# A fused two-group decoder step: the second half of the prompt laid out as the first, and a planner that prices DMA packets and queue slots

## The chip, the cores and the metric

One core of one Trainium2 chip. The time is the device time of one execution in microseconds, the median of the runs shown.

## What is computed

One decoder layer (`DEPTH` is 1) for two groups of requests that share weights: a prompt of 1024 rows and eight single sampled rows with 512 past positions each. Width 1024, feed-forward width 2816, all float32.

```
h = x + 0.5 * rmsnorm(swiglu(rmsnorm(x), gate1, up1, down1))
P = rmsnorm(h) @ w_in                    # 1024 -> 3328 columns
ya = differential attention, 4 heads     # columns 0..1535 of P: q, k, v, rotary on 16 of 64 dims
yb = RWKV-7 time mixing, 8 heads of 64   # columns 1536..3327: token shift, decay, matrix state, group norm
h = h + rmsnorm(concat(ya, yb) @ w_out)
y = h + 0.5 * rmsnorm(swiglu(rmsnorm(h), gate2, up2, down2))
```

The sampled rows attend over a paged cache (`cache_k[page_table]`, `cache_v[page_table]`) and carry their own RWKV state; beside the two `y` the kernel returns the new keys, values, states and last projected rows.

## The kernel before

The prompt is cut into two halves of 512 columns; the eight sampled columns ride along in phase 0 and in phase 3 (520 columns each, the other two phases 512). The feed-forward work is a **trunk** of four phases: phase 0 is FFN 1 of the first half, phase 1 FFN 1 of the second half, phase 2 FFN 2 of the first half, phase 3 FFN 2 of the second half. Between FFN 1 and FFN 2 of a half lies its mixer: the projection `w_in` (stream `proj`, 26 weight tiles), four RWKV jobs (`job`, two at a time), the attention (`prep`, `attn`, `fin`), and `w_out` (`out` for the first half, `outb` for the second). So the mixer of the first half runs beside the trunk of phase 1, and that of the second half beside the trunk of phase 2. The sampled rows have two decoders of their own: `dec` (attention over the cache) and then `decb` (RWKV step).

Every float32 product is three matmuls in fp32r: the weights and the activations are split into a high part and the rest (`split`, `pair`, `mm3`). A weight tile therefore comes in by one 512 KB DMA on SP, is cast by ScalarE, and VectorE or GpSimd subtracts the cast from the original (`wts_w`, `lin_w`). In phases 0 and 3 the trunk has four weight tiles and most gate/up products go by a seven-product scheme on blocks (`sums`, `seven`); in phases 1 and 2 it has two, `w0` and `w1`, and the RWKV jobs use `w2`, `w3`.

The order of the instructions on each engine is made by a **planner** in the program itself. Each stream is a generator (`s_trunk`, `s_weights`, `s_project`, `s_job`, ...) that puts operations into queues; `Kern.put` works out what each depends on, `Kern.price` gives a cost, and `Kern.run` (from L481) picks the next operation: of those ready first, the one with the earliest due time. Due times come from `latest`, which goes backwards over the last plan. `kernel` makes `PASSES` plans in a dry run, takes the one with the shortest planned time, and emits it; the engines then run their instructions in this order. `BIAS = {"trunk2": 300}` sets all due times of the trunk's phase 2 300 us later.

The tiles that the change is about:

- `dreg` (4160 floats a partition): the cache pages and scratch of `dec`, then all scratch of `decb`, later the low halves of the second half's attention operands (`a_buffers`). In phase 1 it also holds the activations of the first `LEAD` = 4 trunk tiles.
- `xl0`, `xl1`: `xl1` is the ring of the trunk's activations, `xl0` the sum of its down products (`self.ytile`).
- `T0`, `T1`: normed input of phases 1 and 3; RWKV job buffers and attention operands of the second half. `X0`, `X1` are the same for the first half.
- `T2`, `T3`: staging tiles (`stage`).

**How the first half is laid out** (s_weights, s_trunk, s_tail, s_project; phase 0 to 1). The residual is read ahead into a free tile (`s_resid`), the normed output goes to `T2`/`T3`, and the operand of the projection to `xl0`/`xl1`. That is possible since phase 1 starts with four gate/up tiles whose activations go to `dreg`; they fill TensorE while the tail is worked out. Then the weight stream stops: the 26 tiles of `w_in` take `w0`, `w1`, and the trunk goes on after them, with a new ring in `xl1`. The job buffers `X0`, `X1` are free at once, so jobs start beside the projection. The first decoder waits for `lead`, the point in phase 1 (group 2, after the down products of group 1) from which `dreg` is free.

**How the second half is laid out.** The residual comes by `hres` DMAs inside the tail (`post`, from L809), the tail works in place in `xl0`, and the operand of the projection goes to `T0`/`T1`. The weights of `w_in` go through `lraw`/`LT` to `w2`, `w3`, beside the trunk of phase 2, which goes on in its ring from its first tile. The job buffers of the second half are the same `T0`, `T1`, so `s_mix` waits for `proj1` (the end of the projection) before it gives them out (L1557). `decb` starts once `dec` is through and has `dreg` from then on. The second half's attention waits for the jobs, the rotary step and `dec_b`, the end of `decb`.

`wide` is true in phases 1 and 2; `cut(t, 4)` makes four places for activations of a tile `t`; `places` names the weight tiles of a linear stream and what frees them.

Of the kernel before, what the change touches and what calls it, by code (L numbers as in the profile page):

```python
# [22 lines left out]
P = 128  # L23
# [72 lines left out]
PASSES = 4  # L96
BIAS = {"trunk2": 300}
# [118 lines left out]
class Kern:  # L216
# [167 lines left out]
    def price(o, op, a, k, out, ins):  # L384
# [5 lines left out]
        if "dma" in op:  # L390
# [9 lines left out]
            o.dma = n * out.shape[0] * 4 / run * max(run * (1 + (run < 512)), 157) / 360e3  # L400
# [80 lines left out]
    def run(self):  # L481
# [4 lines left out]
        rings, tile, size, credit, paced = 0.0, None, None, 0.0, 0.0  # L486
        while self.streams:
# [321 lines left out]
    def post(self, rb, y, gain, o, z=None, rs=None, res=None):  # L809
# [4 lines left out]
        for k in range(KT):  # L814
            if rs is None and k % 2 == 0:
                r = self.residual(n)
                nc.sync.dma_start(r, (self.res if res is None else res)[:, k:k + 2, o:o + n])
# [42 lines left out]
    def s_weights(self):  # L860
# [3 lines left out]
        for ph in range(4):  # L864
# [152 lines left out]
    def s_trunk(self):  # L1017
# [3 lines left out]
        for ph in range(4):  # L1021
# [11 lines left out]
            act = cut(self.T(self.pool, [P, W_DEC], "dreg", FR), 4) if ph == 1 else cut(ring, 4)  # L1033
# [28 lines left out]
            def up(f, c):  # L1062
# [117 lines left out]
            for gi, grp in enumerate(groups):  # L1180
                for q, f in enumerate(grp):
# [11 lines left out]
                    if ph == 1 and f == LEAD:  # L1193
# [49 lines left out]
    def s_tail(self, ph, c, acc, y):  # L1243
# [25 lines left out]
        self.post(norm, y, f"n_ffn{1 + ph // 2}_post", h0 + o, z, rs, self.I["xT"] if ph == 1 else None)  # L1269
        self.signal(("posted" if c else "post", ph))  # L1270
        if ph < 2:
            for t, k in ((self.ytile, 0),) if ph else ((self.zt[0], 0), (self.zt[1], 4)):
                self.keep(ph, c, t, k)
            y = z or y
# [1360 lines left out]
```

## Time and profile before

| | us |
|---|---|
| median of 3 runs | 2288.88 |
| lowest, highest | 2285.25, 2290.93 |
| profiled execution, its own time | 2291.46 |
| span of its profile, first to last instruction | 2289.5 |
| TensorE (PE) busy | 2211.9 (97%) |
| VectorE (DVE) busy | 1539.8 (67%) |
| ScalarE (ACT) busy | 1084.8 (47%) |
| GpSimd (POOL) busy | 977.3 (43%) |
| mean granted TensorE clock | 0.984 |

The first lines of a window table are the stretch in us, its length, and then for each engine the busy time with the number of instructions; then the granted TensorE clock (1 is full speed), the busy share of the 16 DMA engines and what they moved. All operations have the line of one helper (L323), so the tiles' names tell the work: `proj_m<-tail_T,lin_w` is a matmul of the projection into a PSUM bank of the `m` set, with operand `tail_T` and weight `lin_w`. A timeline row has the start, the length, the engine, the operation, and in square brackets how long the engine had been idle and what ended that.

### The profile page before, as it was taken

The numbers are of one execution on the slowest core, as the hardware profiler recorded it, in microseconds if no ns is written. First come the engines' busy times: TensorE is split into PE (matmuls) and PEld (weight loads), VectorE is DVE, ScalarE is ACT, GpSimd is POOL, SyncE is SP. The second block draws the span as 40 slices with busy tenths as digits, with TensorE's granted clock in tenths as the row PEclk, the third lists the DMA queues.
The fourth block names the chain that finished last, engine by engine and source line by source line (L and its number), as shares of the span: only waits on it lengthen the run. The fifth ranks groups of instructions, "written<-read, shape, count | busy, mean of one in ns | idle before, by whom it ended". The sixth has DMA issues, their size and how long they took to land.

```text
span 2289.5 us, 42336 instructions
## 1 busy us (share of the span) xinstructions
PE 2211.9 (97%) x15671; PEld 1970.4 (86%) x15671; DVE 1539.8 (67%) x3573; ACT 1084.8 (47%) x2233; POOL 977.3 (43%) x818
## 2 busy tenths in 40 slices
PE   8999998999999899999899999999999979999998
PEld 8999998898887677988787877777788879999998
DVE  7748887746676587378657566655676356777775
ACT  6524344644553455443552255543576465544444
POOL 4525555533332665464442123333453254444443
PEclk9999999999999999999999999989999989999999
DMA  7322233444343656455568643423644847433433
GB/s 256 109 93 93 84 111 121 135 147 125 110 118 108 177 170 223 138 191 172 162 199 218 184 148 113 111 74 114 196 123 132 278 144 258 152 112 119 148 139 112
DMA packets 241799, 338.75 MB, mean 148 GB/s; under 512 B 78970, under 2 KB 160314, under 8 KB 241594
## 3 DMA queue, kind: packets, MB, share of 16 engines
q1 hardware_dynamic: 241306, 335.53, 46.8%
q8 instruction: 124, 2.03, 0.4%
q14 instruction: 81, 0.66, 0.1%
q10 hardware_dynamic: 288, 0.52, 0.1%
HBM read 281.01 MB, written 54.98 MB: 147 GB/s over the span
## 4 chain that ended last, share of the span: by engine, by line
PE 80%; DVE 7%; DMA 5%; ACT 4%; issue 2%; POOL 1%; SPq 1%; DVEq 0%; ACTq 0%; POOLq 0%
PE trunk_m L323 46%; PE proj_m L323 12%; PE trunk_aux L323 8%; PE job_aux L323 5%; PE out_m L323 2%; PE outb_m L323 2%; PE attn_m L323 2%; DVE mix_T L323 2%; PE attn_aux L323 1%; ACT mix_T L323 1%; SPq L323 1%; PE job_dec L323 1%; DVE trunk_xl L323 1%; PE job_cb L323 1%; DMA mix_T<-out_dram 1%
## 5 line engine op out<-in xcount | busy, mean ns | idle before, releaser
L323 POOL TENSOR_TENSOR wts_w<-wts_raw,wts_w 128x1024 fp32r<-128x1024 f32 (+2 forms) x154 | 293.0, 1909 | 439.0 <-ACT wts_w L323 390.0
L323 PE MATMUL trunk_m<-trunk_xl,wts_w 128*128 128x256 f32 (+2 forms) x2700 | 459.7, 321 | 8.1 <-DVE trunk_xl L323 7.7
L323 PE MATMUL trunk_m<-pre_X,wts_w 128*128 128x512 f32 (+3 forms) x2400 | 441.1, 336 | 12.7 <-ACT wts_w L323 5.5
L323 PEld LDWEIGHTS trunk_m<-trunk_xl,wts_w 128*128 128x128 f32 x2700 | 381.5, 189 | 43.4 <-DVE trunk_xl L323 5.6
L323 PEld LDWEIGHTS trunk_m<-pre_X,wts_w 128*128 128x128 f32 x2400 | 354.1, 191 | 54.7 <-DVE trunk_g L323 6.0
L323 PE MATMUL trunk_m<-pre_T,wts_w 128*128 128x512 f32 (+3 forms) x1848 | 361.8, 349 | 7.7 <-DVE trunk_xl L323 7.7
L323 ACT CAST wts_w<-wts_raw 128x1024 fp32r<-128x1024 f32 (+3 forms) x299 | 244.6, 834 | 217.5 <-PE trunk_m L323 131.7
L323 PEld LDWEIGHTS trunk_m<-pre_T,wts_w 128*128 128x128 f32 x1848 | 291.6, 193 | 46.1 <-issue 9.0
L323 DVE TENSOR_TENSOR trunk_xl<-trunk_xl,trunk_m 128x256 f32<-128x256 f32 (+2 forms) x351 | 165.5, 490 | 60.4 <-PE trunk_m L323 59.1
L323 PE MATMUL proj_m<-tail_xl,lin_w 128*128 128x256 f32 (+1 forms) x1248 | 164.9, 288 | 0.0
L323 PE MATMUL proj_m<-tail_T,lin_w 128*128 128x512 f32 (+1 forms) x672 | 151.7, 384 | 8.9 <-DVE tail_T L323 6.3
L323 PEld LDWEIGHTS proj_m<-tail_xl,lin_w 128*128 128x128 f32 x1248 | 153.5, 188 | 7.7 <-issue 6.4
L323 PEld LDWEIGHTS proj_m<-tail_T,lin_w 128*128 128x128 f32 x672 | 122.3, 193 | 36.4 <-DVE tail_T L323 7.1
L323 POOL TENSOR_TENSOR trunk_xl<-trunk_t,trunk_xl 128x512 fp32r<-128x512 f32 (+3 forms) x85 | 89.0, 1048 | 150.2 <-ACT trunk_xl L323 149.8
L323 DVE TENSOR_TENSOR wts_w<-wts_raw,wts_w 128x1024 fp32r<-128x1024 f32 (+3 forms) x115 | 117.2, 1024 | 26.1 <-ACT wts_w L323 21.6
L323 POOL TENSOR_TENSOR lin_w<-lin_raw,lin_w 128x1024 fp32r<-128x1024 f32 x22 | 53.7, 2442 | 106.5 <-ACT lin_w L323 93.5
L323 ACT CAST wts_w<-wts_lraw 128x512 fp32r<-128x512 f32 x94 | 55.7, 619 | 68.0 <-DMA wts_lraw<-in_ffn_down_dram 34.4
L323 DVE TENSOR_TENSOR trunk_t<-trunk_g,trunk_m 128x512 f32<-128x512 f32 (+2 forms) x75 | 42.1, 562 | 59.1 <-PE trunk_m L323 52.3
L323 POOL TENSOR_TENSOR wts_w<-wts_lraw,wts_w 128x512 fp32r<-128x512 f32 x43 | 59.8, 1392 | 44.8 <-ACT wts_w L323 39.7
L323 DVE SCALAR_TENSOR_TENSOR trunk_g<-trunk_t,trunk_m 128x512 f32<-128x512 f32 (+2 forms) x52 | 32.4, 624 | 61.5 <-ACT trunk_t L323 61.2
L323 PE MATMUL trunk_aux<-trunk_xl,wts_w 128*128 128x256 f32 (+1 forms) x516 | 71.3, 283 | 0.0
L323 PE MATMUL trunk_m<-comb_T,wts_w 128*128 128x260 f32 x540 | 69.7, 283 | 0.0
(619 smaller groups left out, 4196.8 us busy)
## 6 DMA issues: line engine op xcount, KB each, us to landing
wts_raw<-in_ffn_gate_dram SPq DMA_DIRECT2D x87, 512.0 KB
wts_raw<-in_ffn_up_dram SPq DMA_DIRECT2D x58, 512.0 KB
wts_raw<-in_ffn_down_dram SPq DMA_DIRECT2D x56, 384.0 KB
wts_raw<-in_ffn_down_dram SPq DMA_DIRECT2D x29, 512.0 KB
lin_raw<-in_w_in_dram SPq DMA_DIRECT2D x26, 512.0 KB
wts_w<-Ld SPq DMA_DIRECT2D x22, 512.0 KB
mix_T<-out_dram SPq DMA_DIRECT2D x36, 256.0 KB
Ld<-wts_w SPq DMA_DIRECT2D x24, 384.0 KB
```

What stands on the lines that cost most here:

```text
L323: o = Op(eng, lambda: fn(*a, **k), st)
```

## The change

In the second half, what differed from the first is made the same, by turning conditions on phase 0 or 1 into conditions on both halves:

- the residual of phase 1's tail is read ahead by `s_resid`; the tail works into `T2`/`T3` (after phase 2's input is staged) and puts the projection's operand into `xl0`/`xl1`;
- phase 2 starts with four gate/up tiles into `dreg`, after a new wait for `dec_a`, the end of `dec`; the weight stream then waits until the last `w_in` tile is loaded, and the trunk goes on with a new ring in `xl1`; its first down products wait for `proj1`;
- `s_project` of the second half uses `w0`, `w1` and the trunk's two `raw` tiles, after the fourth up tile is loaded; it no longer waits for `outw`;
- `s_mix` gives out the job buffers of the second half without a wait for `proj1`;
- `decb` additionally waits for `lead2`, the point of phase 2 that `lead` (now `lead1`) is in phase 1.

In the planner, a DMA costs `9 + 0.041 * run` nanoseconds for each packet of `run` bytes on one of 16 engines; an operation of SP with a DMA can't start before one of eight places is free, and holds it until 0.1 us after landing; `BIAS` is emptied, and `PASSES` goes from 4 to 8.

```diff
-PASSES = 4
-BIAS = {"trunk2": 300}
+PASSES = 8
+BIAS = {}
...
-            o.dma = n * out.shape[0] * 4 / run * max(run * (1 + (run < 512)), 157) / 360e3
+            o.dma = n * out.shape[0] * 4 / run * (9 + 0.041 * run) / 16e3
...
+        lanes = deque([0.0] * 8)
...
-                        c.append((max(free[e], o.ready + o.load, held[OTHER[e]] if o.port else 0.0), st.prio[e] if o.late is None else o.late, o))
+                        c.append((max(free[e], o.ready + o.load, held[OTHER[e]] if o.port else lanes[0] if o.dma and e != "gpsimd" else 0.0), st.prio[e] if o.late is None else o.late, o))
...
                 o.seen = rings + LAND
+                if o.eng != "gpsimd":
+                    lanes.append(o.seen + 0.1)
+                    lanes.popleft()
...
-                if ph == 1 and n == 2 * LEAD:
-                    yield ("wait", ("loaded", ("in", 0), 25))
-                    last |= {tag: ("used", ("in", 0), 24 + i) for i, tag in enumerate(tags)}
+                if ph in WIDE and n == 2 * LEAD:
+                    yield ("wait", ("loaded", ("in", ph - 1), 25))
+                    last |= {tag: ("used", ("in", ph - 1), 24 + i) for i, tag in enumerate(tags)}
...
-            act = cut(self.T(self.pool, [P, W_DEC], "dreg", FR), 4) if ph == 1 else cut(ring, 4)
+            if ph == 2:
+                yield ("wait", "dec_a")
+            act = cut(self.T(self.pool, [P, W_DEC], "dreg", FR), 4) if wide else cut(ring, 4)
...
-                        if ph == 0:
+                        if ph < 2:
                             self.spawn(self.s_resid(ph), "resid", 0)
...
-                    if ph == 1:
-                        yield ("wait", "proj0")
+                    if wide:
+                        yield ("wait", f"proj{ph - 1}")
...
-                    if ph == 1 and f == LEAD:
+                    if wide and f == LEAD:
                         ring = self.T(self.big, [P, 4160], "xl1", FR)
...
-                        if ph == 1 and gi == 2:
-                            self.signal("lead")
+                        if wide and gi == 2:
+                            self.signal(f"lead{ph}")
...
-        if ph == 0:
+        if ph < 2:
             yield ("wait", ("resid", ph))
             rs = self.rs[c][0]
             if c == 0:
+                if ph:
+                    yield ("wait", ("staged", 2))
                 self.zt = self.stage()
...
-                if ph == 0:
-                    yield ("wait", ("posted", 0))
-                self.px = self.parts(ph, *(self.two(1) if ph else [self.T(self.big, [P, 4160], f"xl{j}", FR) for j in range(2)]))
+                yield ("wait", ("posted", ph))
+                self.px = self.parts(ph, *[self.T(self.big, [P, 4160], f"xl{j}", FR) for j in range(2)])
...
-        if half:
-            yield ("wait", ("outw", 0))
-        else:
-            yield ("wait", ("loaded", 1, "up", LEAD - 1, None))
-            places = ("w0", "w1"), [("used", 1, kind, LEAD - 1, None) for kind in ("gate", "up")]
+        yield ("wait", ("loaded", 1 + half, "up", LEAD - 1, None))
+        places = ("w0", "w1"), [("used", 1 + half, kind, LEAD - 1, None) for kind in ("gate", "up")]
...
-            if half:
-                yield ("wait", "proj1")
             self.job_buffers(half, j)
...
+        self.signal("dec_a")
 
     def s_decode_b(self):
         yield ("wait", "proj0")
+        yield ("wait", "lead2")
```

More of the change, by code (lines that the diff above doesn't have):

```diff
@@ L807, in residual, with post @@
         return r.rearrange("p (j t) -> p j t", j=2)
-    def post(self, rb, y, gain, o, z=None, rs=None, res=None):
+    def post(self, rb, y, gain, o, z=None, rs=None):
         z = z or y
@@ L816, in post @@
                 r = self.residual(n)
-                nc.sync.dma_start(r, (self.res if res is None else res)[:, k:k + 2, o:o + n])
+                nc.sync.dma_start(r, self.res[:, k:k + 2, o:o + n])
             nc.vector.scalar_tensor_tensor(z[k], y[k], self.vec(gain, k), rb, ALU.mult, ALU.mult)
@@ L1256, in s_tail @@
             if c == 0:
+                if ph:
+                    yield ("wait", ("staged", 2))
                 self.zt = self.stage()
             z = [a + b for a, b in self.parts(ph, *self.zt)][c]
-        else:
+        if ph:
             for what in (f"jobs0_{ph - 1}", f"jobs1_{ph - 1}", f"rope{ph - 1}"):
@@ L1268, in s_tail @@
             nc.vector.tensor_tensor(norm, norm, rb, ALU.mult)
-        self.post(norm, y, f"n_ffn{1 + ph // 2}_post", h0 + o, z, rs, self.I["xT"] if ph == 1 else None)
+        self.post(norm, y, f"n_ffn{1 + ph // 2}_post", h0 + o, z, rs)
         self.signal(("posted" if c else "post", ph))
         if ph < 2:
-            for t, k in ((self.ytile, 0),) if ph else ((self.zt[0], 0), (self.zt[1], 4)):
+            for t, k in ((self.zt[0], 0), (self.zt[1], 4)):
                 self.keep(ph, c, t, k)
-            y = z or y
+            y = z
             if c:
@@ L1445, in s_project @@
         nc = self.nc
-        places = None
         for c in range(2):
             yield ("wait", ("prb", half, c))
-        if half:
-            yield ("wait", ("outw", 0))
-        else:
-            yield ("wait", ("loaded", 1, "up", LEAD - 1, None))
-            places = ("w0", "w1"), [("used", 1, kind, LEAD - 1, None) for kind in ("gate", "up")]
+        yield ("wait", ("loaded", 1 + half, "up", LEAD - 1, None))
+        places = ("w0", "w1"), [("used", 1 + half, kind, LEAD - 1, None) for kind in ("gate", "up")]
         job = [16, 12, 20]
@@ L1943, in s_decode_a @@
         yield ("wait", ("done", 0, 3))
-        yield ("wait", "lead")
+        yield ("wait", "lead1")
         if SWAP:
@@ L1951, in s_decode_a @@
             self.spawn(self.s_decode_b(), "decb", 1, "dec", ahead=8)
+        self.signal("dec_a")
     def s_decode_b(self):
         yield ("wait", "proj0")
+        yield ("wait", "lead2")
         if SWAP:
             yield ("wait", "setup")
-            yield ("wait", "lead")
+            yield ("wait", "lead1")
         take = self.arena(self.T(self.pool, [P, W_DEC], "dreg"))
```

## The prediction

> **What bounds the kernel now.** I read the page's busy row and chain first, then a window table cut at the borders of the stages, then the timeline where that table showed idle time.
>
> ```profile
> span 2289.5 us, 42336 instructions
> PE 2211.9 (97%) x15671; PEld 1970.4 (86%) x15671; DVE 1539.8 (67%) x3573; ACT 1084.8 (47%) x2233; POOL 977.3 (43%) x818
> ```
>
> TensorE is the bound on the whole, and the change takes no matmul away. So it can win only what TensorE loses: idle time, and busy time at a lower granted clock. The window table has both (first pair of numbers: length and PE busy; after the POOL column the granted clock, then the DMA share). The first four rows are the first half's layout, the next seven the second half's and what follows it.
>
> ```profile
> 355.00:405.00 50.00, 43.80 (x324) 42.14 (x323) 35.96 (x77) 21.23 (x41) 21.90 (x23) 0.93 0.40 131
> 435.00:655.00 220.00, 218.64 (x2027) 201.40 (x2026) 139.33 (x446) 101.48 (x185) 73.74 (x58) 1.00 0.42 126
> 655.00:745.00 90.00, 88.53 (x712) 68.87 (x710) 54.49 (x168) 41.58 (x96) 27.92 (x23) 1.00 0.40 115
> 745.00:890.00 145.00, 131.77 (x652) 102.78 (x651) 109.00 (x233) 74.70 (x204) 95.34 (x64) 0.96 0.62 188
> 1100.00:1150.00 50.00, 40.30 (x297) 38.16 (x296) 31.36 (x62) 28.12 (x58) 23.47 (x27) 0.90 0.55 175
> 1150.00:1330.00 180.00, 179.14 (x846) 146.69 (x845) 107.18 (x154) 59.70 (x81) 51.49 (x36) 1.00 0.67 189
> 1203.00:1291.00 88.00, 88.00 (x385) 70.38 (x384) 64.34 (x86) 21.89 (x25) 23.68 (x13) 1.00 0.87 223
> 1330.00:1500.00 170.00, 163.56 (x1195) 126.28 (x1194) 117.95 (x391) 93.35 (x185) 62.63 (x40) 1.00 0.44 127
> 1500.00:1615.00 115.00, 112.69 (x785) 88.01 (x784) 60.42 (x181) 46.23 (x102) 35.91 (x25) 0.93 0.32 92
> 1615.00:1866.00 251.00, 248.68 (x1479) 212.73 (x1478) 145.77 (x319) 151.31 (x363) 102.06 (x75) 1.00 0.61 192
> 1866.00:1925.00 59.00, 43.63 (x307) 41.68 (x306) 38.09 (x73) 34.14 (x65) 30.95 (x44) 0.83 0.48 160
> 1925.00:2262.00 337.00, 337.00 (x2806) 336.95 (x2805) 251.09 (x533) 149.91 (x311) 147.26 (x140) 1.00 0.41 145
> ```
>
> I count a row's loss as idle time plus busy time times the missing clock. Second half: border into phase 2 (1100:1150) 9.7 + 0.10 x 40.3 = 13.7; projection and jobs (1150:1330, 1330:1500, 1500:1615) 0.9 + 6.4 + 2.3 + 0.07 x 112.7 = 17.5; attention and `w_out` 2.3; border into phase 3 (1866:1925) 15.4 + 0.17 x 43.6 = 22.8. Together 56.3 us. Phase 3 itself has none. The first half: border 6.2 + 0.07 x 43.8 = 9.3; projection and jobs 1.4 + 1.5 = 2.9.
>
> The timeline shows what the borders wait for.
>
> ```profile
> 1127.97 2.40 PE L323 MATMUL trunk_m<-trunk_xl,wts_w 128*128 128x256 f32 x18 [0.21 <-DVE trunk_xl L323]
> 1132.90 0.38 PE L323 MATMUL proj_m<-tail_T,lin_w 128*128 128x256 f32 x1 [2.53 <-ACT tail_T L323]
> 1139.55 7.75 PE L323 MATMUL proj_m<-tail_T,lin_w 128*128 128x256 f32 x45 [6.27 <-DVE tail_T L323]
> ```
> ```profile
> 1879.01 1.22 PE L323 MATMUL stats_dec<-bset_bv,init_onesD 128*128 128x256 f32 x2 [7.92 <-DVE bset_bv L323]
> 1883.22 8.30 PE L323 MATMUL trunk_m<-pre_X,wts_w 128*128 128x256 f32 x48 [2.99 <-DVE trunk_g L323]
> ```
> ```profile
> 1916.60 8.78 PE L323 MATMUL trunk_m<-pre_T,wts_w 128*128 128x264 f32 x48 [3.23 <-DVE trunk_xl L323]
> ```
>
> At 1130.4 phase 1 is over, and TensorE waits for the tail's operand `tail_T`. At 1871 phase 2 has one tile left and TensorE waits for the statistics of the second half's `w_out` result: the chain jobs, attention, `w_out`, norm ends at the same time as the trunk that should cover it.
>
> **The change part by part.**
>
> *Border into phase 2.* Four gate/up tiles now stand between the last down product and the projection, as in the first half. Its row prices it: 9.3 in place of 13.7, **-4.4**. The residual's 2 MB come ahead of the tail beside the last down weights, by four DMAs on SP in place of these eight; the first half's row holds that too.
>
> ```profile
> tail_hres<-in_xT_dram SPq DMA_DIRECT2D x8, 256.0 KB
> ```
>
> The new wait for `dec_a` I cost at nothing. Queued behind it are the whole of phase 2's trunk and, through the weight stream, the projection; TensorE would have only the tail left.
>
> ```profile
> 1100.81 0.25 DVE L323 SCALAR_TENSOR_TENSOR dec_dreg<-dec_dreg,init_cols 128x32 f32<-128x32 f32 x1
> ```
>
> `dec` is through with `dreg` at 1101, 29 us before phase 2 starts at 1130.4. If that cover goes, every microsecond of it is one of the total.
>
> *Projection and jobs.* The jobs lose the wait for `proj1` and run beside the projection, as in 435:655. Loss 2.9 in place of 17.5, **-14.6**. Against it stands that the first half's projection took longer beside its jobs:
>
> ```profile
> L323 PE MATMUL proj_m<-tail_xl,lin_w 128*128 128x256 f32 (+1 forms) x1248 | 164.9, 288 | 0.0
> ```
> ```profile
> L323 PE MATMUL proj_m<-tail_T,lin_w 128*128 128x512 f32 (+1 forms) x672 | 151.7, 384 | 8.9 <-DVE tail_T L323 6.3
> ```
>
> 13.2 us more, of which 2.4 are its 520 columns against 512. The trunk tiles that the jobs leave may win the other 10.8 back, so the cost is 0 to 10.8; I take the middle, **+5.4**.
>
> *The second decoder* moves from beside the projection to beside phase 2's trunk after `lead2`. No row shows that pairing. Below: 1203:1291, its own core at a DMA share of 0.87, lost nothing. Above: 745:890, `dec` beside trunk and attention, lost 13.2 + 0.04 x 131.8 = 18.5 in 145 us, 17 for 136 us of `decb`. The instructions are those of the first row, so I take **+4**.
>
> *Border into phase 3.* Where the chain comes earlier than the trunk does, the waits of 7.92 and 2.99 and their low clock go; what stays is the last wait, 3.23, and about as much for the clock behind it: 6.6 in place of 22.8, **-16.2** at most.
>
> So TensorE's own limit is -4.4 - 14.6 + 5.4 + 4 - 16.2 = **-26**.
>
> *The chain.* It must come earlier by as much, or TensorE idles at the end instead. This is the step to look at, since the change puts `decb` into it: the attention's operands need `dreg`.
>
> ```profile
> 383.71 3.00 PE L323 MATMUL trunk_m<-pre_T,wts_w 128*128 128x256 f32 x24
> ```
> ```profile
> 434.95 0.40 PE L323 MATMUL proj_m<-tail_xl,lin_w 128*128 128x256 f32 x2
> ```
> ```profile
> L323 PE MATMUL trunk_m<-trunk_dreg,wts_w x96: 387/396/505, 654.7 to 736.5; 128*128 128x512 f32 x96
> ```
> ```profile
> 1233.14 76.45 PE proj_m L323 x330
> ```
>
> In the first half the projection starts 51.2 us after the trunk's phase, so now at 1130.4 + 51.2 = 1181.6. `dreg` was last read 301.6 us after that, which gives 1483. But in the 82 us from 654.7 to 736.5 the trunk needed only 216 matmuls (`plan`: down groups 0 and 1 with 72 and 48, two gate/up pairs with 96) at the projection's 76.45 / 330 = 0.232 us each, 50 us; the other 32 were the jobs', and then nothing waited for `dreg`. Now due times put the trunk first: 1483 - 32 = 1451.
>
> ```profile
> 1102.97 0.37 SPq L323 DMA_DIRECT2D decb_dreg<-out_dram  x1
> ```
> ```profile
> 1133.15 0.22 ACT L323 ACTIVATE decb_dreg<-decb_dreg 128x32 f32<-128x32 f32 x1
> ```
> ```profile
> 1149.40 0.30 PE L323 MATMUL decb_dec<-decb_dreg,init_bones 128*128 128x32 f32 x2
> ```
> ```profile
> 1153.46 0.19 DVE L323 TENSOR_TENSOR decb_dreg<-decb_dreg,init_cols 128x32 f32<-128x32 f32 x1
> ```
> ```profile
> 1200.32 0.30 PE L323 MATMUL decb_dec<-decb_dreg,init_bones 128*128 128x32 f32 x2
> ```
> ```profile
> 1290.82 0.69 DVE L323 TENSOR_REDUCE decb_dreg<-decb_dreg 128x8 f32<-128x512 f32 x1
> ```
> ```profile
> 1326.29 0.30 PE L323 MATMUL decb_dec<-decb_dreg,init_bones 128*128 128x32 f32 x2
> ```
> ```profile
> 1336.25 0.38 SPq L323 DMA_DIRECT2D YM<-decb_dreg  x1
> ```
>
> `decb` took 1103.0 to 1336.6, 234 us. Three times its next matmul, which needed nothing but the row before, came late: 16, 47 and 35 us. Nothing was waiting for it then. Without them it is 136 us.
>
> ```profile
> L323 PE MATMUL job_aux<-bset_sg,bset_g x8: 592/592/675, 1437.2 to 1612.9; 128*128 128x512 f32 x8
> ```
> ```profile
> 1618.39 0.48 PE L323 MATMUL attn_aux<-mix_T 128*128 128x320 f32 x2
> ```
>
> The attention started 5.5 us after the last job. Now: 1451 + 136 + 5.5 = 1592.5, **26 us earlier** than 1618.4. The jobs are no limit: from the end of the projection at 1330 they took 283 us, and as long from 30 us into the projection they end near 1495. Both limits come out at 26. Where they meet, each still delays the other; I give back a good third of the 10.9 us of waits at 1871 to 1883, 4 us: **-22**.
>
> *The plan.* Four more passes and the empty `BIAS` cost no instruction. The new order reaches the whole program, but 1925:2262 has nothing left to win; for the rest I allow 8 us either way, a little over half of the 13.2 idle in 745:890. The packet price can be checked on the stretch of `decb`:
>
> ```profile
> DMA packets 33484, 19.59 MB, mean 223 GB/s; under 512 B 29329, under 2 KB 29361, under 8 KB 33478
> ```
> ```profile
> q1 hardware_dynamic: 33478, 19.51, 86.5%
> ```
>
> Measured: 0.865 x 88 = 76.1 us of each engine. New price: (33478 x 9 + 19.51e6 x 0.041) / 16 = 68.8 us. The plan thus takes this stretch, nearly all packets of 256 bytes, for 7 us shorter than it is. The Trainium skill ("DMA: Bandwidth & Descriptors", Specifications) says that below 512 bytes the engines do a read-modify-write and miss line rate, which is the step that the old price had and the new one drops; by that rule, and this row agrees in sign, the attention starts some 7 us later than planned and the gain would be 15 in place of 22.
>
> **The rivals.**
>
> *No change.* The trunk keeps the first half's pace to `lead2`, and only `decb` hurries: 1483 + 136 + 5.5 = 1624.5, 6 us later than now. What TensorE saves at 1130 and 1500 is then idle time at 1870, and the time is 2289 + 6 = 2295. For it: the pace is a measured one. Against it: then nothing waited for `dreg`.
>
> *Slower: the decoder is last.* `decb` starts at 1451 but keeps two of its late matmuls, since each is one in a queue of trunk matmuls and its result goes through a busy VectorE: 136 + 16 + 35 = 187, attention at 1643.5, 25 us later, and the end with it: 2314. It decides from a `decb` of 169 us on (1618.4 + 7 - 5.5 - 1451). For it: the change ties a step of many small DMAs and short vector work, which had 1618 - 1337 = 281 us to spare, into the only chain that ends at phase 3. Against it: the plan knows that and sets its due times by it.
>
> *The layout does less than it says*: the first half's clean rows came from its plan and not from the layout, and the second half's jobs, in step with each other, lose the clock again as in 1500:1615: 7.9 of the 14.6 stay. The chain still comes 26 earlier: about 2275, inside my range.
>
> **How the numbers follow.** The profiled execution took 2291.5, 2.6 above the median of 2288.9; I apply -22 to the median: **2267**. Chances: the forecast with its variants 0.60, no change 0.17, decoder last 0.23. The likeliest case's own range is 2246 (no cost of `decb`, nothing given back, 8 from the new order: -42) to 2281. The whole range goes on through the no-change case to 2306, short of the slower case's 2314 and what lies above it, some 0.12; below 2246 I leave 0.06. A measurement tells 0.3%, about 7 us, from no change: faster 0.60, same 0.17, slower 0.23.
>
> **What would show it.** Right: no wait for `tail_T` at 1130 to 1150; job matmuls from about 1210 on among the projection's; `trunk_m<-trunk_dreg` a second time, ending near 1451; `decb` right after it, done near 1590; the attention's first matmul near 1593; no wait over 5 us before phase 3. Wrong: `decb` over 169 us, a gap of TensorE before phase 3 longer than now, the first activation of phase 2 waiting for `dec_dreg`, or a clock below 1 between 1181 and 1500.

## The result and the profile after

| | median, us | lowest to highest | runs |
|---|---|---|---|
| before | 2289.9 | 2285.25 to 2294.97 | 4 |
| after | 2262.68 | 2260.26 to 2266.19 | 4 |

The ratio is 0.9882 (95% interval 0.9856 to 0.9907): 27 us less. The first two lines of the page of after, then its window table, cut at its own borders of the stages (length and TensorE busy first; after the POOL column the granted clock):

```profile
span 2261.8 us, 42336 instructions
...
PE 2204.0 (97%) x15671; PEld 1961.9 (87%) x15671; DVE 1561.4 (69%) x3583; ACT 1078.3 (48%) x2222; POOL 983.4 (43%) x817
```
```profile
745.00:890.00 145.00, 138.45 (x703) 109.58 (x702) 111.65 (x244) 77.98 (x210) 99.87 (x64) 1.00 0.67 199
1100.00:1170.00 70.00, 66.96 (x412) 59.16 (x411) 51.48 (x80) 41.57 (x78) 41.37 (x44) 1.00 0.62 212
1170.00:1360.00 190.00, 188.91 (x1247) 146.41 (x1245) 117.93 (x303) 85.43 (x153) 69.28 (x40) 1.00 0.42 130
1360.00:1452.00 92.00, 88.70 (x661) 69.94 (x659) 66.87 (x228) 44.44 (x98) 26.11 (x17) 1.00 0.46 133
1452.00:1582.00 130.00, 129.84 (x685) 101.11 (x684) 82.44 (x169) 44.67 (x78) 41.27 (x24) 1.00 0.67 171
1582.00:1755.00 173.00, 171.29 (x954) 142.02 (x953) 128.27 (x266) 107.40 (x292) 75.24 (x45) 1.00 0.49 148
1755.00:1840.00 85.00, 84.99 (x556) 77.20 (x556) 36.12 (x61) 42.97 (x72) 32.71 (x34) 1.00 0.79 268
1840.00:1896.00 56.00, 42.36 (x309) 39.98 (x308) 37.81 (x74) 34.51 (x66) 28.81 (x42) 0.88 0.46 149
```

TensorE's idle time fell from 77.6 (2289.5 - 2211.9) to 57.8 us (2261.8 - 2204.0), its busy time by 7.9: 19.8 + 7.9 = 27.7, the whole difference of the spans. From 1100 to 1840 only 9.3 us are lost in all; two thirds of what is left of the second half's losses are in the last row, the border into phase 3: 13.6 idle + 0.12 x 42.4 = 18.7 us. And 745:890, in a stage whose layout the change does not touch, loses 6.6 where it lost 18.5.

The timeline at the two borders of after, first into phase 2, then into phase 3:

```profile
1111.73 4.56 PE L323 MATMUL trunk_m<-trunk_xl,wts_w 128*128 128x256 f32 x37
1116.13 0.59 PE L323 MATMUL tail_aux<-trunk_acc,init_onesD 128*128 128x256 f32 x2
1117.37 2.86 PE L323 MATMUL trunk_m<-pre_X,wts_w 128*128 128x256 f32 x22 [0.64 <-ACT wts_w L323]
```
```profile
1872.51 7.48 PE L323 MATMUL trunk_m<-trunk_xl,wts_w 128*128 128x256 f32 x45 [7.14 <-DVE trunk_xl L323]
1880.20 4.53 PE L323 MATMUL trunk_m<-trunk_xl,wts_w 128*128 128x256 f32 x36 [0.21 <-DVE trunk_xl L323]
1884.57 0.59 PE L323 MATMUL last_aux<-trunk_acc,init_onesD 128*128 128x256 f32 x2
1884.81 2.48 PE L323 MATMUL trunk_m<-trunk_xl,wts_w 128*128 128x256 f32 x18
1889.71 7.47 PE L323 MATMUL trunk_m<-pre_T,wts_w 128*128 128x264 f32 x47 [2.42 <-DVE trunk_xl L323]
```

Phase 2 begins 0.6 us after phase 1; no wait for the tail is left. Phase 3 begins at 1889.7 in place of 1916.6, 26.9 earlier, with a wait of 7 us a little ahead of it. The chain that leads there:

```profile
L323 PE MATMUL trunk_m<-trunk_dreg,wts_w x96: 387/393/798, 1376.8 to 1451.5; 128*128 128x512 f32 x96
```
```profile
1451.91 0.38 SPq L323 DMA_DIRECT2D decb_dreg<-out_dram  x1
```
```profile
1581.50 0.43 SPq L323 DMA_DIRECT2D YM<-decb_dreg  x1
```
```profile
1582.82 0.48 PE L323 MATMUL attn_aux<-mix_T 128*128 128x320 f32 x2
```
```profile
L323 PE MATMUL outb_m<-outb_T,lin_w x384: 275/283/475, 1754.7 to 1834.6; 128*128 128x264 f32 x96, 128*128 128x256 f32 x96
```

`dreg` is read for the last time at 1451.5, `decb` starts 0.4 us later and ends at 1582, the attention starts there, and `w_out` at 1754.7. The attention starts 35.6 us earlier than before, but `w_out` only 23.6. The trunk's share of TensorE in the attention's stretch shows where the 12 us between the two went (length, then busy time of the trunk's products alone; before, then after):

```profile
1618.40:1778.30 159.90, 106.74 (x395) 71.14 (x394) 18.40 (x27) 2.96 (x5) 1.00 0.51 154
```
```profile
1582.80:1754.70 171.90, 119.16 (x447) 80.58 (x446) 19.81 (x29) 3.57 (x6) 1.00 0.49 147
```

What is not trunk is the same, 53.2 and 52.7 us: the attention lasted 12 us longer, and TensorE did 12 us more of the trunk in it. TensorE is busy in nearly the whole stretch, so this does not show which caused which. Trunk products may have stood ahead of the attention's, or have filled its waits for another engine (VectorE's busy time in the stretch rose from 110.5 to 127.3 us).

### The profile page after: what moved, and what is told of

Its sections match the earlier page's. It is cut to its first block, busy times and chain, and to the rows that moved or that the text cites. A ratio compares the mean times of both kernels' runs of the same rounds, so it can differ in the third digit from the quotient of the medians.

```text
span 2261.8 us, 42336 instructions
## 1 busy us (share of the span) xinstructions
PE 2204.0 (97%) x15671; PEld 1961.9 (87%) x15671; DVE 1561.4 (69%) x3583; ACT 1078.3 (48%) x2222; POOL 983.4 (43%) x817
## 5 line engine op out<-in xcount | busy, mean ns | idle before, releaser
L323 PE MATMUL trunk_m<-trunk_xl,wts_w 128*128 128x256 f32 (+2 forms) x2604 | 433.7, 318 | 14.5 <-DVE trunk_xl L323 11.9
L323 PE MATMUL trunk_m<-pre_X,wts_w 128*128 128x512 f32 (+3 forms) x2400 | 430.2, 333 | 9.3 <-ACT wts_w L323 6.5
L323 PEld LDWEIGHTS trunk_m<-trunk_xl,wts_w 128*128 128x128 f32 x2604 | 366.2, 190 | 44.4 <-DVE trunk_xl L323 13.5
L323 PEld LDWEIGHTS trunk_m<-pre_X,wts_w 128*128 128x128 f32 x2400 | 353.1, 190 | 49.7 <-ACT wts_w L323 5.9
L323 PE MATMUL proj_m<-tail_xl,lin_w 128*128 128x256 f32 (+2 forms) x1920 | 327.2, 323 | 0.4 <-POOL lin_w L323 0.4
L323 PEld LDWEIGHTS proj_m<-tail_xl,lin_w 128*128 128x128 f32 x1920 | 269.7, 188 | 36.6 <-issue 11.5
L323 POOL TENSOR_TENSOR lin_w<-lin_raw,lin_w 128x1024 fp32r<-128x1024 f32 x44 | 106.2, 2414 | 199.5 <-ACT lin_w L323 161.7
L323 ACT CAST lin_w<-lin_raw 128x1024 fp32r<-128x1024 f32 x52 | 54.5, 1047 | 80.3 <-PE proj_m L323 48.1
L323 POOL TENSOR_TENSOR wts_w<-wts_lraw,wts_w 128x512 fp32r<-128x512 f32 x39 | 54.1, 1390 | 35.7 <-ACT wts_w L323 32.3
L323 ACT CAST wts_w<-wts_dec 128x512 fp32r<-128x512 f32 x30 | 17.6, 587 | 107.0 <-DVE wts_dec L323 107.0
L323 PEld LDWEIGHTS trunk_m<-comb_T,wts_w 128*128 128x128 f32 x540 | 66.9, 188 | 0.0
```

The lines of the kernel that those rows point to most:

```text
L323: o = Op(eng, lambda: fn(*a, **k), st)
```

## The experiments

Three questions: which half of the change, layout or plan, makes the gain; does the chain set the end; and which part of the plan matters. Each kernel is compared with before in interleaved runs; differences from after come from the difference of the two ratios (0.0044 is 10 us), and are uncertain by some 7 to 9 us either way.

### Layout and plan apart

`layout_only` is after with the old planner (its diff against after, without the further lines of the lanes); `plan_only` is before with the new one.

```diff
-PASSES = 8
-BIAS = {}
+PASSES = 4
+BIAS = {"trunk2": 300}
...
-            o.dma = n * out.shape[0] * 4 / run * (9 + 0.041 * run) / 16e3
+            o.dma = n * out.shape[0] * 4 / run * max(run * (1 + (run < 512)), 157) / 360e3
...
-        lanes = deque([0.0] * 8)
...
```

> The changed kernel with the planner as before: old packet price, no queue slots, 4 passes, due times of the trunk's phase 2 set 300 us later. Theory S (split): the changed time has two parts. 12 to 14 us come from the new plan's order in the first half, where phase 1 now ends at 1116 in place of 1130 with the same layout; the rest from the second half's layout. Then this kernel ends phase 1 near 1130 and takes 2289.9 - 14 = 2276 (2271 to 2281). Theory L (the layout gives all, as the prediction had it): 2263 to 2268.

> The kernel before with the new planner alone: new packet price, eight queue slots, 8 passes, no bias. Theory S: phase 1 ends near 1116 and all later stages come as much earlier, 2289.9 - 13 = 2277 (2271 to 2283). Theory L: the order of the first half moves the time by no more than 5 us, 2285 to 2295. If the bias of 300 us was needed by the old layout, phase 2's trunk crowds out the jobs and the time is above 2295, with phase 1's end still telling S from L.

| | old plan | new plan |
|---|---|---|
| old layout | 1 | 0.9988 (0.9973 to 1.0003), 2284.27 us |
| new layout | 1.006 (1.0041 to 1.0079), 2301.7 us | 0.9882 (0.9856 to 0.9907), 2262.68 us |

Neither the theory of a split nor that of the layout alone holds. Each half of the change by itself gives nothing or a loss; together they give 27 us. The two rows of `layout_only` (745:890 and the border into phase 2) and its last read of `dreg`:

```profile
745.00:890.00 145.00, 132.71 (x656) 103.87 (x656) 107.84 (x235) 74.77 (x205) 94.54 (x62) 0.96 0.64 187
1100.00:1170.00 70.00, 54.73 (x371) 50.53 (x370) 48.14 (x83) 39.67 (x77) 36.79 (x42) 0.90 0.51 160
```
```profile
L323 PE MATMUL trunk_m<-trunk_dreg,wts_w x96: 387/394/795, 1405.7 to 1482.8; 128*128 128x512 f32 x96
```

The same layout loses 15.3 + 0.10 x 54.7 = 20.7 us at the border where after loses 3.0, and frees `dreg` at 1482.8, 31 us later. Over half of the 20.7 is one wait:

```profile
1154.32 1.22 PE L323 MATMUL trunk_m<-pre_X,wts_w 128*128 128x512 f32 x2 [10.93 <-DVE trunk_g L323]
```

The lead tiles are issued there, but TensorE waits 10.9 us until VectorE has worked on one of their results (`trunk_g`). For that it needs a result of ScalarE (`trunk_t`), which comes only at 1153.4; from 1142 to 1152 the plan has ScalarE mostly on the tail (`tail_xl`, `tail_sq`). The clean border was thus not the layout's alone: the four lead tiles fill it only if the plan puts their work on the other engines in time. `plan_only`, same two places of interest (the second is the border into phase 3):

```profile
745.00:890.00 145.00, 139.93 (x710) 111.05 (x709) 112.50 (x249) 79.57 (x212) 102.00 (x64) 1.00 0.64 197
1840.00:1930.00 90.00, 73.57 (x464) 64.73 (x464) 60.30 (x111) 51.63 (x101) 51.92 (x73) 0.83 0.67 233
```

The plan alone does win the first half's stage (a loss of 5.1 in place of 18.5). But in the old layout the second half's attention starts at 1608.4, and 16.4 + 0.17 x 73.6 = 28.9 us are lost ahead of phase 3, against 22.8 before (1866:1925): part of what TensorE saves early it loses again late.

### Does the chain set the end?

`lead_late` (first diff) gives `lead2` one group later. `lead_early` (second) regroups the down products of phases 1 and 2 so that `dreg` is free earlier, and lets the trunk wait for the end of the projection ahead of its fifth tile.

```diff
-                        if wide and gi == 2:
+                        if wide and gi == (2 if ph == 1 else 3):
```
```diff
-        groups = [[0, 1, 2], [3, 4], [5, 6]] + [list(range(g, g + 3)) for g in range(7, NF, 3)]
+        groups = [[0, 1, 2, 3]] + [list(range(g, g + 3)) for g in range(4, NF, 3)]
...
-        return {1: 8, 2: 4, 3: 2}[len(grp)]
+        return {1: 8, 2: 4, 3: 2, 4: 2}[len(grp)]
...
                     if wide and f == LEAD:
+                        yield ("wait", f"proj{ph - 1}")
...
-                        if wide and gi == 2:
+                        if wide and gi == 1:
```

> The changed kernel with the second decoder let in one trunk group later: two gate/up pairs and one down group of two more, 144 matmuls of 0.232 us = 33 us. Theory C (chain): the second half runs from the release of the decoder's tile over the decoder to the attention and to the start of phase 3, and all of these move by 33 us: attention from 1583 to about 1616, time 2262.7 + 33 = 2296 (2285 to 2302). Rival P (TensorE is the bound after the change, the chain has slack): the time stays at 2260 to 2268.

> The changed kernel with phases 1 and 2 grouped 4, 3, 3, 3, 3, 3, 3 in place of 3, 2, 2, 3, 3, 3, 3, 3, so that the first group's down products free the decoder's tile: 144 matmuls stand between the projection and that point in place of 216, 72 x 0.232 = 17 us fewer. Theory C: attention near 1566 in place of 1583, and the time falls by what TensorE still loses at the border into phase 3 (13.6 us idle, 5 at the lower clock) up to 17: 2246 to 2255. Rival P: 2259 to 2265, since only eight accumulations are saved.

`lead_late`: 0.9979 (0.9964 to 0.9995), 22 us above after. Theory P, which had 2260 to 2268, falls; theory C has the direction, but its 2285 to 2302 lies above the 2281.74 measured. `decb` started 15 us later than in after (1467.2), not 33, and was through 19 us later. The attention's first products came at 1593.5, before that; those that read `dreg` came 21 us later than in after (`lead_late` twice, then after):

```profile
1600.63 0.37 SPq L323 DMA_DIRECT2D YM<-decb_dreg  x1
```
```profile
L323 PE MATMUL attn_aux<-mix_dreg,mix_T x16: 304/367/417, 1616.2 to 1775.4; 128*128 128x320 f32 x4, 128*128 128x384 f32 x4, 128*128 128x448 f32 x4, 128*128 128x512 f32 x4
```
```profile
L323 PE MATMUL attn_aux<-mix_dreg,mix_T x16: 304/354/397, 1595.2 to 1742.4; 128*128 128x320 f32 x4, 128*128 128x384 f32 x4, 128*128 128x448 f32 x4, 128*128 128x512 f32 x4
```

So with `decb` through 19 us later the time is 22 us longer: the end of `decb` holds the end here, and not the attention's first product. `lead_early`: 0.9883 (0.9858 to 0.9908), no change, though `dreg` was free at 1420.6, 31 us earlier:

```profile
L323 PE MATMUL trunk_m<-trunk_dreg,wts_w x96: 387/394/792, 1396.7 to 1420.6; 128*128 128x512 f32 x96
```

Here theory C falls (2246 to 2255), and the 2262.45 measured lies in theory P's 2259 to 2265. `decb` started at once, at 1421.1, but took 151 us in place of 130: its input was ready at 1429.6, and its first matmul came only at 1446.1. So 20 of the 31 us were gone before the attention, which began only 9 us earlier, at 1574.1, and lasted 188.7. (The profiled execution took 2274.8 us, 12 above the median, so its late times prove little.) The chain holds the end when it comes later; when its head comes earlier, `decb` takes longer, and what sets the end then is not shown.

`jobs_wait` undoes one part of the layout: the job buffers wait for the end of the projection again.

```diff
         for j in range(2):
+            if half:
+                yield ("wait", "proj1")
             self.job_buffers(half, j)
```

> The changed kernel, but the second half's job buffers are given out only after proj1, the end of the projection, as before the change. Theory C (the chain sets the end): from the end of the projection at 1377 the jobs take the 283 us that they took before, the attention begins near 1665 in place of 1583, and TensorE idles before phase 3 for most of these 82 us: 2315 to 2345. Theory P (the layout wins only what TensorE lost beside the jobs, 14.6 us by the prediction): 2270 to 2282. Theory M (the planner, told of it, hurries the jobs, which have TensorE nearly to themselves after 1377, as in the first half, where the four jobs took 290 us of which 60 were after the projection): the attention begins near 1620 to 1640 and the time is 2290 to 2315.

0.9994 (0.9976 to 1.0013): with this one wait put back, the whole gain is gone (25.6 us). The last job's row in after and in `jobs_wait`:

```profile
L323 PE MATMUL job_aux<-bset_sg,bset_g x8: 590/592/592, 1341.4 to 1526.6; 128*128 128x512 f32 x8
```
```profile
L323 PE MATMUL job_aux<-bset_sg,bset_g x8: 590/591/1055, 1399.9 to 1605.0; 128*128 128x512 f32 x8
```

The jobs end at 1605 and not near 1660; the attention starts at 1611.6, 28.8 later than in after, and the time is 25.6 longer. `decb` was through at 1580.4, so here the jobs hold the attention. The 2285.88 measured lies between theory P's 2270 to 2282 and theory M's 2290 to 2315, and far below theory C's 2315 to 2345: it is theory M's mechanism, hurried jobs, at a smaller price than M gave. The later attention was a later end, nearly one for one.

### Which part of the plan?

Five kernels put one part of the old planner back into after, or two; the diffs are those of `after_bias`, `after_4passes` and `no_slots`. `old_price` has the line of `o.dma` from the first diff above, `layout_8passes` that and no lanes. `plan_only_bias` is the old layout with the new planner and the old bias.

```diff
-BIAS = {}
+BIAS = {"trunk2": 300}
```
```diff
-PASSES = 8
+PASSES = 4
```
```diff
-                        c.append((max(free[e], o.ready + o.load, held[OTHER[e]] if o.port else lanes[0] if o.dma and e != "gpsimd" else 0.0), st.prio[e] if o.late is None else o.late, o))
+                        c.append((max(free[e], o.ready + o.load, held[OTHER[e]] if o.port else 0.0), st.prio[e] if o.late is None else o.late, o))
```

> The changed kernel with BIAS = {"trunk2": 300} put back; layout, packet price, queue slots and eight passes stay. Open is why the new layout with the old planner is 14 us slower than before and with the new planner 25 us faster. Theory B (the bias): due times 300 us later for the whole of phase 2 now also put off its four lead tiles and its first two groups, and these free dreg; decb and the attention come later: 2290 to 2305, with the last matmul on trunk_dreg near 1480 as in the layout with the old planner. Theory D (the DMA model): it is the price and the slots, the bias does little: 2260 to 2272, last matmul on trunk_dreg near 1450. Theory R (a re-roll: any edit of the planner moves the plan by 10 us or so either way, and no part of it is responsible): 2270 to 2290.

> The changed kernel with the old price of a DMA and without the queue slots; layout, empty BIAS and eight passes stay. Theory B: the bias is what hurt, so this is as fast as the changed kernel: 2260 to 2272. Theory D: the plan without the new DMA model takes packets and queue for what they are not; the first half's stage 745 to 890 loses its 13 us again and the end of phase 1 is back near 1128: 2288 to 2302. Theory R: 2270 to 2290.

> The changed kernel with PASSES = 4 in place of 8, nothing else. Theories B and D: 2260 to 2270, the passes are not what matters. Theory R: more passes are more draws, and the gain is the luck of the best one: 2272 to 2290.

> The old layout with the new price, the queue slots and eight passes, but with BIAS = {"trunk2": 300} kept. With the bias emptied the old layout ended phase 2's trunk 80 us before the attention's part was through, and the 20 us that its first half had won went into the gap before phase 3. Theory B: with the bias the trunk of phase 2 covers again, and the first half's gain of 14 to 20 us reaches the end: 2266 to 2278. Theory D the same, but for the 9 us of border that the layout gives: 2270 to 2280. Theory R: 2280 to 2292. If it comes out at 2265 or below, the new layout was worth nothing by itself.

> The changed kernel without the eight queue slots in the plan; the new packet price stays. Without both the time was 18 us above the changed kernel's. Theory S (the slots are what the plan needs, since SP's DMAs wait for a place in the queue): 2276 to 2284, with the loss in 745 to 890 back near 11 us. Theory Q (the price is): 2260 to 2268, the loss in 745 to 890 near 6.6 as in the changed kernel. Theory R: in between, 2268 to 2276.

> The changed kernel with the old price of a packet (full rate above 512 bytes, twice the time below, at least 157 bytes' worth); the eight queue slots stay. Without the slots alone the time was 18 us above the changed kernel's, without both 23 us above. Theory S (the slots carry it, the price adds little): 2262 to 2270, the attention takes 170 to 178 us. Theory Q (the plan needs both, since the slots hold a place until a landing that the price sets): 2275 to 2284, and the attention takes over 185 us as in the run without slots. Theory K (the prediction's remark on the price: the new one takes decb's packets for 7 us shorter than they are, the old one for longer): decb and the attention are no later than in the changed kernel and the time is 2255 to 2262.

| kernel | median, us | ratio to before (95%) | above after, us |
|---|---|---|---|
| `after_4passes` | 2268.26 | 0.9919 (0.989 to 0.9949) | 8 |
| `after_bias` | 2270.22 | 0.9935 (0.9911 to 0.996) | 12 |
| `old_price` | 2277.0 | 0.9954 (0.9937 to 0.9971) | 16 |
| `no_slots` | 2279.38 | 0.9964 (0.9946 to 0.9982) | 19 |
| `layout_8passes` | 2280.09 | 0.9983 (0.9965 to 1.0002) | 23 |
| `layout_only` (all back) | 2301.7 | 1.006 (1.0041 to 1.0079) | 41 |
| `plan_only_bias` | 2278.5 | 0.9968 (0.9949 to 0.9987) | 20 |

The DMA model (price and slots together) is worth 23 us to the new layout, the bias 12, the passes 8; the sum, 43, is about the 41 of all together. Theory B, the bias alone, falls: without it `layout_8passes` has only a seventh of the gain, and with it `after_bias` is at 2270 and not at 2290 or above. Theory D said 2288 to 2302 for `layout_8passes` and has the direction; the 2280.09 measured lies in theory R's 2270 to 2290, the re-roll, as `after_bias` just does. `after_4passes` lies in the 2260 to 2270 of B and D, and not in R's. `plan_only_bias` is within D's range: the old layout, best planned, is still 20 us behind. Price and slots are not worth their sum (16 + 19 against 23): one without the other can't be told from neither. The times are those of theory S for `no_slots` (2276 to 2284) and of theory Q for `old_price` (2275 to 2284); theory S for `old_price` (2262 to 2270) and theory K, on the price, fall. Theory S's reason for `no_slots`, that SP's DMAs wait for a place in a queue, is shown by no trace here. The 8 us of the passes do not stand out of the uncertainty.

Where does the DMA model's share show? Hardly where I looked for it: `no_slots` loses 9.6 us in 745:890 against 6.6. One part is `decb`, which is through 8 to 9 us later than in after, where this row stands at 1581.50 (`no_slots`, then `old_price`):

```profile
1589.93 0.38 SPq L323 DMA_DIRECT2D YM<-decb_dreg  x1
```
```profile
1590.15 0.38 SPq L323 DMA_DIRECT2D YM<-decb_dreg  x1
```

The rest lies between that and `w_out`, 192 and 177 us in place of 173. The stretch from the attention's first product to `w_out` (trunk products alone; `no_slots`, then `old_price`):

```profile
1584.90:1781.80 196.90, 140.63 (x538) 97.29 (x537) 24.60 (x36) 4.17 (x7) 1.00 0.47 147
```
```profile
1585.80:1767.30 181.50, 129.09 (x492) 89.22 (x492) 21.18 (x31) 4.20 (x7) 1.00 0.51 148
```

The attention's first products come within 3 us of after's 1582.8 in both, but those that read `dreg` at 1607.0 and 1603.1, 12 and 8 us later; and the stretch lasts 197 and 182 us in place of 172. 21 of the 25 us in the first, 10 of the 10 in the second are more trunk products inside it. As above, this does not show whether the trunk delayed the attention or filled its waits, nor why the price and the slots decide it. Each edit of the planner gives a new order of the whole program, and the runs don't separate a better model from a luckier order.

### The bias where it doesn't hurt

The bias puts phase 2's trunk late, the lead tiles too. `split_bias` keeps it only behind `lead2`.

```diff
-BIAS = {}
+BIAS = {"trunk2": 300}
...
-            o.late += BIAS.get(st.part, 0) + sum(...)
+            o.late += BIAS.get(st.part, 0) * ("lead2" in self.signals) + sum(...)
```

> The changed kernel with the due times of phase 2's trunk put 300 us later again, but only for what the trunk issues after lead2; the four lead tiles and the first two groups keep their own. With the bias on all of phase 2 the stretch 1100 to 1170 lost 16.7 us in place of 3.0, while the attention took 168 us in place of 171 and began 1 us earlier; four runs without the bias had attentions of 177 to 194 us. Theory B2 (the bias hurts at the border and helps the attention): the stretch 1100 to 1170 keeps a clock of 1.00 and a loss of 3 to 5, the attention takes 160 to 168 us and ends near 1745, and the time is 2250 to 2260, below the changed kernel. Theory B1 (a wrong due time hurts wherever it is): 2266 to 2276. Theory R (every edit of the planner re-rolls the whole order by some 5 us): 2258 to 2270 with no pattern in the two stretches.

The border into phase 2 in `after_bias`, then in `split_bias`, and the stretch 1840:1896 of `split_bias`:

```profile
1100.00:1170.00 70.00, 59.18 (x321) 51.14 (x320) 47.63 (x70) 38.83 (x70) 34.73 (x39) 0.90 0.53 168
```
```profile
1100.00:1170.00 70.00, 66.85 (x409) 58.83 (x409) 52.17 (x80) 41.23 (x78) 40.83 (x43) 1.00 0.60 205
1840.00:1896.00 56.00, 49.69 (x375) 47.99 (x374) 37.03 (x68) 37.24 (x68) 31.60 (x42) 0.94 0.49 163
```

`split_bias` has the median of 2257.43 us, 0.9871 (0.9846 to 0.9897): the lowest of all: 15 us below `after_bias`, but only 2.5 below after, from which it can't be told apart. The border is clean again (3.2 in place of 16.7), as B2 said. The attention did not get shorter, against B2: it lasted 176 us. It started at 1563.4, 19 us earlier, since `decb` ended at 1560. Of these 19 us phase 3 saw 4: it began at 1885.7. 1840:1896 lost 6.3 + 0.06 x 49.7 = 9.3 in place of 18.7, so with an earlier chain the border does shrink towards the 6.6 of the prediction, and TensorE's own work begins to be the limit.

## Why the prediction was right, point by point

*The time.* 2267 forecast, 2262.68 measured, faster. The mechanism, that TensorE loses some 26 us less and the chain comes some 26 us earlier, is seen in after: `w_out` starts 23.6 us earlier and phase 3 26.9. But the prediction gave it to the layout, and the layout by itself does not do it: `layout_only` is 14 us slower than before. The terms differ from mine as follows, loss by the rule of the prediction, from the rows of before and after.

| term | forecast | measured |
|---|---|---|
| border into phase 2 | -4.4 | 3.0 for 13.7: -10.7 |
| projection and jobs | -14.6 | 1.1 + 3.3 = 4.4 for 17.5: -13.1 |
| longer projection | +5.4 (0 to 10.8) | +10.6 |
| `decb` beside the trunk | +4 (0 to 17) | +0.2 |
| attention and `w_out` | 0 | 1.7 for 2.3: -0.6 |
| border into phase 3 | -16.2 at most | 18.7 for 22.8: -4.1 |
| the plan in the first half (355 to 1100) | 0, 8 either way | -10.3, of which 745:890 is 6.6 for 18.5: -11.9 |

The last column adds up to -28.0 against the 27.7 of the spans; stretches that are not listed differ by under 2 us. The forecast's terms, without the plan, add up to -26. One by one the seven miss by 40 us in all, and their sum by 2 (the -22 on record, with 4 given back, by 5): that it came so near is luck. The range's lower end is not what its items give, either (22 + 4 + 4 + 8 is 38 and not 42), but nothing hangs on it. The longer projection stood at its upper bound: its one row in after has 327.2 us, the two of before 164.9 + 151.7 = 316.6.

```profile
L323 PE MATMUL proj_m<-tail_xl,lin_w 128*128 128x256 f32 (+2 forms) x1920 | 327.2, 323 | 0.4 <-POOL lin_w L323 0.4
```

*The mis-sized term* is the border into phase 3. I let it fall by 16.2 to its last wait, 6.6 us, if the chain came earlier than the trunk did. It fell by 4.1. TensorE was near the end of phase 2's products before the chain was at its own, and the wait of 7.1 us for `trunk_xl`, which ends at 1872.5, is a wait for the chain's last step. VectorE works on the normed input of phase 3 (`pre_T`, made from the result of `w_out`) before it takes the next sums of down products, which TensorE had done by 1863.8:

```profile
1861.90 0.36 DVE L323 TENSOR_TENSOR trunk_xl<-trunk_xl,trunk_m 128x256 f32<-128x256 f32 x1
1863.37 0.48 DVE L323 SCALAR_TENSOR_TENSOR pre_T<-pre_sq,init_cols,pre_T 128x256 fp32r<-128x256 f32 x1 [1.11 <-ACT pre_T L323]
...
1870.59 0.48 DVE L323 SCALAR_TENSOR_TENSOR pre_T<-pre_sq,init_cols,pre_T 128x256 fp32r<-128x256 f32 x1 [0.29 <-ACT pre_T L323]
...
1872.04 0.74 DVE L323 TENSOR_TENSOR trunk_xl<-trunk_xl,trunk_m 128x256 f32<-128x256 f32 x2
```

So the forecast's sign "no wait over 5 us before phase 3" did not come. What the border kept, the first half gave: the new plan took 12 us off 745:890 alone, where I had allowed 8.

*The chain.* `dreg` free at 1451, measured 1451.5, but by two errors that cancel: phase 1 ended 14 us earlier than I took (1116 for 1130.4), and the trunk then did not hurry by 32 us but by some 18. From the end of the projection it still took 75 us, 82 in the first half, where I had 50; the other 11 or so lay ahead of that end. `decb` took 130 us for 136. The attention followed 1 us after it and not 5.5, which makes 1582.8 for my 1592.5. Those 10 us went into the attention, 12 longer, which I had left at its old length. The jobs ended at 1526.6, 32 us later than my 1495, and were no limit.

*The new wait for `dec_a`* cost nothing, as priced: the first products of phase 2 come at 1117.4, 0.6 us behind phase 1, and `dec` had been through with `dreg` at 1108.6.

*The price of packets.* `decb`'s stretch in after, 1452 to 1582, DMA packets:

```profile
DMA packets 41229, 22.19 MB, mean 171 GB/s; under 512 B 34171, under 2 KB 37658, under 8 KB 41219
```
```profile
q1 hardware_dynamic: 41219, 22.07, 66.3%
```

Measured: 0.663 x 130 = 86.2 us of each engine; the new price gives (41219 x 9 + 22.07e6 x 0.041) / 16 = 79.7. The plan is 6.5 us too short here, as in the prediction's row. Yet `decb` was not late by it: it took 130 us where I had 136, at a DMA share of 0.66. What sets its pace no run here separates. The 15 us of gain that I derived from the Trainium skill's rule ("DMA: Bandwidth & Descriptors", Specifications: below 512 bytes a read-modify-write) did not come; the row agrees with the rule in sign, and no run here shows an effect of it on the time.

*The rivals.* "No change" is what `layout_only` did at its head: the trunk keeps the first half's pace and frees `dreg` at 1482.8 where the rival said 1483. Its end, 2301.7, is also nearest to that rival's 2295, but it did not come that way. `decb` took 123 us and the attention began at 1605.5, 19 us before the rival's 1624.5 and 13 before that of the kernel before. Its profile has 4.4 us more idle time than before and 5.5 more busy time, the latter for a reason not shown. So the rival was right on the pace and not on the chain, and what decided was the plan, to which the prediction gave "8 us either way". "Decoder last" needed a `decb` of 169 us that ends near 1638. It took 130 here; in `lead_early` and `jobs_wait`, where it started earlier, it took 151 and 178, but in no run was it through later than 1606. "The layout does less than it says": the second half's jobs kept a clock of 1.00, and its premise was right in part: a clean row needs the plan as well as the layout.

*The step that a reader should doubt* is thus the treatment of the plan as an allowance beside the layout. With the new layout the plan was worth 41 us, with the old one 3.

## What to carry to other kernels

When a program orders its own instructions by a plan, a change of layout and a change of the plan are one change: measure all four combinations before giving either the credit, since the same layout cost 14 us under one plan and won 24 under the other here. TensorE's savings ahead of a border count only as far as the chain that ends there comes earlier too; what one of the two gains beyond the other shows up as a wait at that border. And look at what shares the engines with the last serial stage: in the four stretches shown, what is not trunk kept to 52 to 56 us of TensorE, while the attention took 160 to 197 us with the trunk's products inside it. At two borders TensorE waited 7 and 11 us while VectorE or ScalarE did another stage's work ahead of the trunk's: the order on an engine that is not the bottleneck can decide.

## What the runs showed of the hardware

The wait of 7 us before phase 3 costs more than itself. Windows of some 3.4 us of after (length, TensorE busy, granted clock):

```profile
1863.08:1866.50 3.42, 1.62 (x13) 1.00 0.62 196
1866.10:1869.50 3.40, 0.00 (x0) 0.56 0.00 0
1869.50:1872.90 3.40, 0.39 (x2) 0.50 0.00 0
1872.90:1876.30 3.40, 3.40 (x17) 0.50 0.02 5
1876.30:1879.70 3.40, 3.40 (x28) 0.93 0.64 211
```

TensorE stands still from 1865.4, and the clock is at half from about 1866.5. TensorE starts again at 1872.5 and is fully busy in the fourth row, at half clock: 17 products in place of 28. So some 4 us of work run at half speed behind the wait. The Trainium skill ("TensorE: Matmul & The Clock Gate", Part 1) says that after an idle window the clock is half until one window of about 3.4 us was busy; the last two rows agree with the second part of it. With the first part they do not quite: the 3.4 us ahead of the fall, the first row, were not idle, since TensorE was busy for 1.62 of them.
